# HGRN level products on four column tiles and RWKV state queries inside the state steps of a hybrid decoder layer

## The chip, the cores and the metric

The kernel runs on one core of one Trainium2 chip. Its time is the device time of one execution in microseconds; the runs shown are three of the unchanged kernel. The engines are called by the profile's names: PE is TensorE (PEld its weight loads), DVE VectorE, ACT ScalarE, POOL GpSimd and SP SyncE. The profile comes from one execution of its own.

## The reference

One decoder layer on 2048 tokens of width 1024, all in float32. A joint input projection feeds two mixers that lie side by side: HGRN2 with four heads of 128 columns, and RWKV-7 with eight heads of 64. Their outputs are joined and projected back, and a ConvFFN follows.

```python
def step(S, inp):                        # HGRN2, chunks of 64 tokens
    qb, kb, vb, gb = inp
    b = jnp.cumsum(gb, axis=2)
    diff = b[:, :, :, None, :] - b[:, :, None, :, :]
    dec = jnp.exp(jnp.where(causal, diff, -jnp.inf))
    A = jnp.einsum('bhtk,bhsk,bhtsk->bhts', qb, kb, dec)
    o = jnp.einsum('bhts,bhsv->bhtv', A, vb) + jnp.einsum('bhtk,bhkv->bhtv', qb * jnp.exp(b), S)
    ...

def step(S, inp):                        # RWKV-7, one token
    rt, wt, kt, vt, at, bt = inp
    sa = jnp.einsum('bhvk,bhk->bhv', S, at)
    S = S * wt[:, :, None, :] + sa[..., None] * bt[:, :, None, :] + vt[..., None] * kt[:, :, None, :]
    y = jnp.einsum('bhvk,bhk->bhv', S, rt)
    return S, y
```

RWKV's y is normalised over each head of 64 (mean and variance), scaled by ln_w and shifted by ln_b, gets a bonus term, and is multiplied by a gate.

## The kernel before

The layer is written with a tile framework: the program names tiles and operations, and a planner at build time sets the order of each engine's instructions. It goes by the order of the program and by its own costs, and may put a later instruction first where an earlier one is not ready by those costs. On the chip each engine then runs its own list in order.

The tokens are worked in four blocks of 512. Three generators give out the mixer stage: `dense` (projections, as products of high and low float32r parts, L263 to L265), `rw_stream` (RWKV) and `hg_stream` (HGRN). A loop takes one step of RWKV and one of HGRN and then dense work worth `TICK`, 2000 ns by the program's own costs; call this a round. A step ends at a `yield`.

**HGRN.** `hg_unit` handles one head in one block, 16 times in all. Decay within 128 tokens is handled in seven levels: level l pairs the first half of each group of 2 x 2^l tokens with the second half. `scaled(l)` multiplies queries and keys by the decay that belongs to the level, `level` multiplies them on TensorE (L979), and `take` copies the entries that belong to the level out of PSUM by a mask into the score matrix A (L985). The diagonal (query and key of the same token) is a product of its own. Before the change a block of 64 keys is stationary, 128 rows by 64 columns, and two such blocks go to the two column tiles at columns 0 and 64. Queries that do not take part at a level are skipped, so 32 columns stream past at a level and 64 for the diagonal. Diagonal and levels 0 to 2 form a first run of products, levels 3 to 5 a second; level 6, between the two halves of 128 tokens, is L1023. A is then copied to the two diagonal blocks of Af, whose product with the values is L1041.

**RWKV.** `rw_super` handles two pairs of heads (u = 0, 1; the two heads of a pair lie in partitions 0 to 63 and 64 to 127) in one block, eight times in all. What the change touches:

- Scores (L723): for j in 0, 1 and each pair u, eight products into one PSUM tile (`bank2`, of which two exist), two masked multiplications (L726) that read it, and a `yield`. The multiplication at L711 makes the operand, L712 the one behind it.
- The eight state steps: four state products a step (L894, one for each u and head, 64x64, at the quadrants (0, 0) and (64, 64)) add to `xp`; VectorE scales the result to the next state XH (L896); `yield`.
- The part of y that does not need the state goes to `yp` at L884 beforehand. Behind the eight steps the state queries (L904) add XH times RT to `yp`, 32 products, at the same two quadrants as the state products.
- Then y is squared, averaged by a product with ones on each block of 64, normalised, scaled and shifted by two ScalarE instructions (one for each u), added to the bonus, multiplied by the gate and stored.

A float32 product leaves two records in the trace; a transpose and a float32r product leave one.

Of the kernel before, what the change touches and what calls it, by code (L numbers as in the profile page):

```python
# [7 lines left out]
F32 = mybir.dt.float32  # L8
F32R = mybir.dt.float32r
BF16 = mybir.dt.bfloat16  # L10
U32 = mybir.dt.uint32
AF = mybir.ActivationFunctionType
# [6 lines left out]
P = 128  # L19
# [10 lines left out]

C_CEN, C_ONE, C_S1, C_DG = 0, 128, 256, 384
C_LV = 448
C_SCAN = C_LV + 6 * 64
C_PAR = C_SCAN + 512
C_ID = C_PAR + 2
C_W = C_ID + 128
# [2 lines left out]
def make_consts():  # L39
    import numpy as np  # L40

    c = np.zeros((P, C_W), np.float32)
    p = np.arange(P)[:, None]
    q = np.arange(P)[None, :]
    same = ((p // 64) == (q // 64)).astype(np.float32)
    c[:, C_ID:C_ID + P] = p == q
    for f in range(2):
        c[:, C_PAR + f] = np.arange(P) % 2 == f
    c[:, C_CEN:C_CEN + P] = (p == q) - same / 64.0
    c[:, C_ONE:C_ONE + P] = same  # L50
    t = np.arange(64)[None, :]
    s = p % 64
    c[:, C_S1:C_S1 + 64] = t > s
    c[:, C_S1 + 64:C_S1 + 128] = t >= s
    c[:, C_DG:C_DG + 64] = t == s
    for l in range(6):
        m = 1 << l
        tq = np.arange(64).reshape(-1, 2, m)[:, 1, :].reshape(1, 32)
        c[:, C_LV + 64 * l:C_LV + 64 * l + 32] = ((tq // (2 * m)) == (s // (2 * m))) & ((s // m) % 2 == 0)
    c[:, C_SCAN:C_SCAN + 512] = (np.arange(512) % 64 != 0)[None, :]  # L60
    return c

# [2 lines left out]
def tile_layer(ctx, tc, consts, x, norm1_w, w_in, hg_lb_logits, hg_norm_w, rw_shift_mu, rw_w0, rw_w2,  # L65
# [4 lines left out]
    V, S, TE = nc.vector, nc.scalar, nc.tensor  # L70
    dma, store = nc.sync.dma_start, nc.gpsimd.dma_start

    cp = ctx.enter_context(tc.tile_pool(name="cp", bufs=1, reuse_waits="tile"))
# [16 lines left out]
    blk1 = cst[:, C_ONE:C_ONE + P]  # L90
    s1m = cst[:, C_S1:C_S1 + P]
    dgm = cst[:, C_DG:C_DG + 64]
    scanm = cst[:, C_SCAN:C_SCAN + 512]

    def pst(name):
# [14 lines left out]
    def act(out_, in_, func, **kw):  # L110

        want = tables.get(func)
        if want is not None and want != tab["now"]:
            pre = S.preload_act_table_set(want)
            for u_ in tab["uses"]:
                tc.add_manual_dep(pre.ins, u_.ins.name, NOSYNC, reason="table order")
            tab.update(now=want, pre=pre, uses=[])
        i_ = S.activation(out_, in_, func, **kw)  # L118
        if want is not None:
            tc.add_manual_dep(i_.ins, tab["pre"].ins.name, NOSYNC, reason="table order")  # L120
            tab["uses"].append(i_)
        return i_
# [12 lines left out]
    off = {}  # L135
    with tc.tile_pool(name="vp", bufs=1, reuse_waits="tile") as vp, tc.tile_pool(name="ps0", bufs=1, space=PSUM, reuse_waits="tile") as pools["ps"]:
        rows = vp.tile([P, P], F32, name="rows")
        V.memset(rows, 0.0)
        n = 0
# [15 lines left out]
    def vec(nm, i):  # L155
        return vt[:, off[nm] + i:off[nm] + i + 1]


    lb = cp.tile([P, 12], F32, name="lb")
    lb0 = vt[:, off["lb"]:off["lb"] + 4]  # L160
# [106 lines left out]
    def phase1(c1):  # L267
# [22 lines left out]
        def bank(kind):  # L290
            return ps.tile([P, 512], F32, tag=kind, name=kind, bufs=2)
# [329 lines left out]
        def last_dma(nb):  # L621

            return nc.gpsimd.dma_start if nb == NBLK - 1 else dma
# [16 lines left out]
        def rw_super(nb, s_):  # L640
# [75 lines left out]
            for j in range(2):  # L716
                for u in U:
                    s1 = bank2()
                    for i in range(4):
                        b, e = 2 * j + i // 2, i % 2  # L720
                        for h in range(2):
                            hr = slice(h * 64, h * 64 + 64)
                            TE.matmul(s1[:, h, i * P:i * P + P], KB[hr, 4 * u + b, 2 * e:2 * e + 2, :],  # L723
                                      AR[hr, u, :, 2 * b + e, :], start=True, stop=True)
                    for h in range(2):
                        V.tensor_mul(M[:, :, u, 2 * j:2 * j + 2, h, :].rearrange("p e b t -> p b e t"),  # L726
                                     s1[:, h].rearrange("p (b e t) -> p b e t", e=2, t=P),
                                     s1m.unsqueeze(1).unsqueeze(1).broadcast_to([P, 2, 2, P]))
                    yield

            E = rp.tile([P, 32, 32], F32, tag="E", name="E")
# [148 lines left out]
            for u in U:  # L880
                for ch in range(8):
                    b, e = ch // 2, ch % 2
                    for h in range(2):
                        TE.matmul(yp[h * 64:h * 64 + 64, u, ch * 64:ch * 64 + 64],  # L884
                                  UV[:, 4 * u + b, e, h * 64:h * 64 + 64], M[:, e, u, b, h, 64:128], start=ch == 0,
                                  stop=False, tile_position=(0, h * 64), skip_group_check=True)
            WC2 = WC.rearrange("p (u c) t -> p u c t", u=2)
            for ch in range(8):
                b, e = ch // 2, ch % 2
                cs_ = slice(ch * 64, ch * 64 + 64)  # L890
                for u in U:
                    for h in range(2):
                        hr = slice(h * 64, h * 64 + 64)
                        TE.matmul(xp[hr, u, cs_], M[hr, 1, u, b, e, 0:64], XH[hr, u, ch, :], start=False,  # L894
                                  stop=ch == 7, tile_position=(h * 64, h * 64), skip_group_check=True)
                V.tensor_mul(XH[:, :, ch + 1, :], xp[:, :, cs_], WC2[:, :, ch].broadcast_to([P, 2, 64]))  # L896
                yield
            V.tensor_copy(Xc[:, 2 * s_:2 * s_ + 2, :], XH[:, :, 8, :])
            for u in U:
                for ch in range(8):  # L900
                    cs_ = slice(ch * 64, ch * 64 + 64)
                    for h in range(2):
                        hr = slice(h * 64, h * 64 + 64)
                        TE.matmul(yp[hr, u, cs_], XH[hr, u, ch, :], RT[hr, u, ch, :], start=False, stop=ch == 7,  # L904
                                  tile_position=(h * 64, h * 64), skip_group_check=True)
            yo = tile_("KB", [2, 2, BLK], "yo")
            y1, y2 = yo[:, 0], yo[:, 1]
            act(y1, yp, AF.Square)
# [5 lines left out]
            act(y1, b1, AF.Ln, bias=epsgn, scale=1.0 / 64)  # L914
            act(y1, y1, AF.Exp, scale=-0.5)
            V.tensor_mul(y2, yp, y1)
            for u in U:
                act(y2[:, u], y2[:, u], AF.Identity, bias=vec("lnb", prs[u]), scale=vec("lnw", prs[u]))
            yield
            while ("gd", nb) not in stage:  # L920
                yield None
# [1 line left out]
            gm = bank2()  # L923
            for u in U:
                TE.matmul(gm[:, u, :], g2[:, pc[u]], gdt, start=True, stop=True)
            V.tensor_add(y2, y2, BV)
            V.tensor_mul(y2, gm, y2)
            last_dma(nb)(oT[nb][512 + prs[0] * P:512 + (prs[1] + 1) * P, :].rearrange("(u p) t -> p u t", p=P), y2)
            done["rw2"] += 1
            yield  # L930

# [1 line left out]
        def hg_unit(nb, j):  # L933
# [7 lines left out]
                TE.transpose(tp[:, b * P:(b + 1) * P], v[:, b * P:(b + 1) * P], ident)  # L941
            act(VT, tp.rearrange("p (b t) -> p b t", t=P), AF.Copy)
            yield
            A = rp.tile([P, 4, 64], F32, tag="hA", name="A")
            Pf = f
            Sf = rp.tile([P, BLK], F32, tag="Sf", name="Sf")
            V.memset(Sf.rearrange("p (n e) -> p n e", e=2)[:, :, 1:2], 1.0)
# [18 lines left out]

            def level(lp, off, kt, qt, l=None):

                w = 64 if l is None else 32
                for b in range(4):  # L970
                    for e in range(2):
                        t0 = (2 * b + e) * 64
                        qs = qt[:, t0:t0 + 64]
                        o = lp[e * 64:e * 64 + 64, off + b * w:off + b * w + w]
                        if l is not None:
                            m = 1 << l
                            qs = qs.rearrange("p (n e m) -> p n e m", e=2, m=m)[:, :, 1, :]
                            o = o.rearrange("p (n m) -> p n m", m=m)
                        TE.matmul(o, kt[:, t0:t0 + 64], qs, start=True, stop=True, tile_position=(0, e * 64))  # L979

            def take(l, lp, off):

                m = 1 << l
                mk = cst[:, C_LV + 64 * l:C_LV + 64 * l + 32].bitcast(U32).rearrange("p (n m) -> p n m", m=m)
                V.copy_predicated(A.rearrange("p b (n e m) -> p b n e m", e=2, m=m)[:, :, :, 1, :],  # L985
                                  mk.unsqueeze(1).broadcast_to([P, 4, 32 // m, m]),
                                  lp[:, off:off + 128].rearrange("p (b n m) -> p b n m", b=4, m=m))

            Xs = []
            for l in range(3):  # L990
                Xs.append(scaled(l))
                yield
            l0, l1 = bank("hg"), bank("hg")
            level(l0, 0, k, q)
            for l in range(3):
                level(l1, l * 128, Xs[l], Xs[l], l)
            V.tensor_mul(A, l0[:, 0:256].rearrange("p (b t) -> p b t", t=64), dgm.unsqueeze(1).broadcast_to([P, 4, 64]))
            for l in range(3):
                take(l, l1, l * 128)
            yield  # L1000
            Xs = []
            for l in range(3, 6):
                Xs.append(scaled(l))
                yield
            l1 = bank("hg")
            for l in range(3, 6):
                level(l1, (l - 3) * 128, Xs[l - 3], Xs[l - 3], l)
            for l in range(3, 6):
                take(l, l1, (l - 3) * 128)
            act(Af[0:64, :, 0:64], A[0:64], AF.Copy)  # L1010
            act(Af[64:128, :, 64:128], A[64:128], AF.Copy)
            yield
            X = scaled(6)
            V.tensor_mul(k, k, Sf)
# [587 lines left out]
```

## Time and profile before

| | us |
|---|---|
| runs | 2671.83, 2675.3, 2676.13 (median 2675.3) |
| profiled execution, span from first to last instruction | 2678.7 |
| TensorE busy in the span | 2595.9 (97%) |
| VectorE busy | 1964.4 (73%) |
| ScalarE busy | 1368.4 (51%) |
| HGRN level products (L979, 32 streamed columns), busy | 52.2 |
| HGRN diagonal (L979, 64 columns) | 11.9 |
| RWKV scores (L723) | 37.9 |
| RWKV state products (L894) | 30.2 |
| RWKV state queries (L904) | 18.8 |

For the profiled execution the page gives the span and no other time. Busy time of a group is the union of its instructions' times; products overlap in the pipeline, so a product's own duration (about 0.22 us) is far longer than the distance from one start to the next. In a timeline the columns are start, time covered, engine, line, operation, output and inputs by tile, shapes and count; neighbouring instructions of one kind are merged into one row.

### The profile page before, as it was taken

The numbers are of one execution on the slowest core, as the hardware profiler recorded it, in microseconds if no ns is written. First come the engines' busy times: TensorE is split into PE (matmuls) and PEld (weight loads), VectorE is DVE, ScalarE is ACT, GpSimd is POOL, SyncE is SP. The second block draws the span as 40 slices with busy tenths as digits, with TensorE's granted clock in tenths as the row PEclk, the third lists the DMA queues.
The fourth block names the chain that finished last, engine by engine and source line by source line (L and its number), as shares of the span: only waits on it lengthen the run. The fifth ranks groups of instructions, "written<-read, shape, count | busy, mean of one in ns | idle before, by whom it ended". The sixth has DMA issues, their size and how long they took to land. (4 is left out here: it accounts for less than half of the span.)

```text
span 2678.7 us, 47929 instructions
## 1 busy us (share of the span) xinstructions
PE 2595.9 (97%) x18059; PEld 2089.1 (78%) x18059; DVE 1964.4 (73%) x3744; ACT 1368.4 (51%) x2200; POOL 383.2 (14%) x686
## 2 busy tenths in 40 slices
PE   7999999999999999999999999999999999999998
PEld 5877777777777777778778888887888888888887
DVE  4877767676567675667678789988998888676556
ACT  4556453554545455344457655456555545545444
POOL 6433222212222123222100000000000000000000
PEclk9999999999999999999999999999999999999999
DMA  8654443355643546844584458756754463898665
GB/s 301 202 164 165 163 142 116 115 162 183 201 152 115 153 157 221 277 131 129 172 287 139 138 188 262 239 172 194 260 199 150 149 203 124 318 322 280 204 193 185
DMA packets 312702, 510.54 MB, mean 191 GB/s; under 512 B 46879, under 2 KB 143509, under 8 KB 312469
## 3 DMA queue, kind: packets, MB, share of 16 engines
q1 hardware_dynamic: 257937, 329.13, 37.3%
q0 software_dynamic: 54464, 178.32, 20.4%
q8 instruction: 142, 2.33, 0.4%
q14 instruction: 91, 0.75, 0.1%
q10 hardware_dynamic: 68, 0.02, 0.0%
HBM read 373.13 MB, written 134.22 MB: 189 GB/s over the span
## 5 line engine op out<-in xcount | busy, mean ns | idle before, releaser
L263 PE MATMUL pj<-hh,wh 128*128 128x512 f32 x960 | 394.1, 411 | 6.7 <-ACT rkv L118 1.6
L264 PE MATMUL pj<-hl,wh 128*128 128x512 f32 x960 | 377.9, 394 | 0.0
L265 PE MATMUL pj<-hh,wl 128*128 128x512 f32 x960 | 377.7, 394 | 0.0
L263 PE MATMUL ua<-Bh,uwh 128*128 128x512 f32 x704 | 276.1, 392 | 3.8 <-ACT m L118 2.6
L265 PE MATMUL ua<-Bh,uwl 128*128 128x512 f32 x704 | 274.3, 390 | 0.0
L264 PE MATMUL ua<-Bl,uwh 128*128 128x512 f32 x704 | 274.1, 389 | 0.0
L263 PEld LDWEIGHTS pj<-hh,wh 128*128 128x128 f32 x960 | 181.1, 189 | 56.6 <-issue 9.1
L265 PEld LDWEIGHTS pj<-hh,wl 128*128 128x128 f32 x960 | 181.0, 189 | 39.6 <-issue 0.2
L264 PEld LDWEIGHTS pj<-hl,wh 128*128 128x128 f32 x960 | 181.3, 189 | 34.3 <-issue 0.6
L247 ACT CAST uwh<-uraw 128x512 fp32r<-128x512 f32 x220 | 135.2, 618 | 137.7 <-PE ua L264 63.3
L248 DVE TENSOR_TENSOR dal<-draw,dah 128x512 fp32r<-128x512 f32 x138 | 95.3, 690 | 111.3 <-ACT dah L247 110.0
L248 DVE TENSOR_TENSOR uwl<-uraw,uwh 128x512 fp32r<-128x512 f32 x220 | 147.5, 687 | 35.0 <-ACT uwh L247 34.9
L247 ACT CAST dah<-draw 128x512 fp32r<-128x512 f32 x138 | 85.9, 622 | 163.7 <-PE da L264 79.1
L263 PEld LDWEIGHTS ua<-Bh,uwh 128*128 128x128 f32 x704 | 132.1, 188 | 33.2 <-ACT m L118 4.8
L265 PEld LDWEIGHTS ua<-Bh,uwl 128*128 128x128 f32 x704 | 132.2, 188 | 28.1 <-DVE uwl L248 0.4
L264 PEld LDWEIGHTS ua<-Bl,uwh 128*128 128x128 f32 x704 | 132.2, 188 | 26.8
L263 PE MATMUL ud<-Bh,uwh 128*128 128x512 f32 x352 | 138.0, 392 | 0.0
L265 PE MATMUL ud<-Bh,uwl 128*128 128x512 f32 x352 | 137.0, 389 | 0.0
L264 PE MATMUL ud<-Bl,uwh 128*128 128x512 f32 x352 | 137.0, 389 | 0.0
L1472 POOL DMA_DIRECT2D gd<-y x2 | 1.1, 542 | 945.3 <-DVE y L1470 945.3
L264 PE MATMUL da<-dbl,dah 128*128 128x512 f32 x332 | 129.4, 390 | 0.3 <-DVE dbl L248 0.2
L265 PE MATMUL da<-dbh,dal 128*128 128x512 f32 x332 | 129.2, 389 | 0.0
(580 smaller groups left out, 6268.9 us busy)
## 6 DMA issues: line engine op xcount, KB each, us to landing
uraw<-in_w_up_dram SPq DMA_DIRECT2D x176, 256.0 KB, 3.3
woraw<-in_w_out_dram POOLq DMA_DIRECT2D x96, 256.0 KB, 3.4
br<-gd SPq DMA_DIRECT2D x88, 256.0 KB, 4.0
draw<-Sg SPq DMA_DIRECT2D x88, 256.0 KB, 2.8
draw<-Tw SPq DMA_DIRECT2D x88, 256.0 KB, 3.1
gd<-y SPq DMA_DIRECT2D x86, 256.0 KB, 2.8
Sg<-br SPq DMA_DIRECT2D x72, 256.0 KB, 2.1
xt<-x1d SPq DMA_DIRECT2D x32, 512.0 KB, 6.1
```

The lines of the kernel that those rows point to most:

```text
L247: S.copy(hi, src)
L248: V.tensor_sub(lo, src, hi.bitcast(F32))
L263: TE.matmul(acc, lh, rh, start=first, stop=False, skip_group_check=skip)
L264: TE.matmul(acc, lh, rl, start=False, stop=False, skip_group_check=skip)
L265: TE.matmul(acc, ll, rh, start=False, stop=last, skip_group_check=skip)
L1472: (dma if end is None else nc.gpsimd.dma_start)(gd_[2 * h + b][fb * P:(fb + 1) * P, :], ys[0][:, b * BLK:(b + 1) * BLK])
```

## The change

**HGRN.** A block of 32 keys is now stationary, 128 rows by 32 columns, and four such blocks go to the four column tiles at columns 0, 32, 64 and 96. A level streams 16 queries past each, the diagonal 32. A is 32 columns wide in place of 64. The levels 0 to 4 stay inside such blocks; level 5, between two blocks of 32, becomes `across`, eight products on the column tiles 0 and 64 whose result ScalarE copies from PSUM straight to Af. The diagonal shares a PSUM tile with levels 0 to 2. The masks in the constants shrink in the same way.

**RWKV scores.** For each j both pairs' products and masked multiplications come first, then two yields.

**RWKV state queries.** They move into the state steps, four behind each step's four state products. The second pair's results go to the other column half (`c0 = (h ^ u) * 64`), so the four of a step use all four quadrants, and in `yp` the two heads of the second pair lie exchanged. The scaling by the norm's weights puts them back: two ScalarE instructions of 64 partitions each, with weights exchanged in the same way (`lnx`, copied once at the start). From there y1 takes the place of y2.

```diff
+    lnx = cp.tile([P, 4], F32, name="lnx")
+    for r0 in (0, 64):
+        S.copy(lnx[r0:r0 + 64, :], vt[64 - r0:128 - r0, off["lnw"] + 1:off["lnw"] + 8:2])
...
                         V.tensor_mul(M[:, :, u, 2 * j:2 * j + 2, h, :].rearrange("p e b t -> p b e t"),
...
+                for _ in U:
                     yield
...
-                        TE.matmul(yp[h * 64:h * 64 + 64, u, ch * 64:ch * 64 + 64],
+                        c0 = (h ^ u) * 64
+                        TE.matmul(yp[c0:c0 + 64, u, ch * 64:ch * 64 + 64],
                                   UV[:, 4 * u + b, e, h * 64:h * 64 + 64], M[:, e, u, b, h, 64:128], start=ch == 0,
-                                  stop=False, tile_position=(0, h * 64), skip_group_check=True)
+                                  stop=False, tile_position=(0, c0), skip_group_check=True)
...
+                for u in U:
+                    for h in range(2):
+                        hr, c0 = slice(h * 64, h * 64 + 64), (h ^ u) * 64
+                        TE.matmul(yp[c0:c0 + 64, u, cs_], XH[hr, u, ch, :], RT[hr, u, ch, :], start=False,
+                                  stop=ch == 7, tile_position=(h * 64, c0), skip_group_check=True)
                 V.tensor_mul(XH[:, :, ch + 1, :], xp[:, :, cs_], WC2[:, :, ch].broadcast_to([P, 2, 64]))
                 yield
             V.tensor_copy(Xc[:, 2 * s_:2 * s_ + 2, :], XH[:, :, 8, :])
-            for u in U:
-                for ch in range(8):
-                    cs_ = slice(ch * 64, ch * 64 + 64)
-                    for h in range(2):
-                        hr = slice(h * 64, h * 64 + 64)
-                        TE.matmul(yp[hr, u, cs_], XH[hr, u, ch, :], RT[hr, u, ch, :], start=False, stop=ch == 7,
-                                  tile_position=(h * 64, h * 64), skip_group_check=True)
...
-            for u in U:
-                act(y2[:, u], y2[:, u], AF.Identity, bias=vec("lnb", prs[u]), scale=vec("lnw", prs[u]))
+            act(y1[:, 0], y2[:, 0], AF.Identity, bias=vec("lnb", prs[0]), scale=vec("lnw", prs[0]))
+            for r0 in (0, 64):
+                rs_ = slice(64 - r0, 128 - r0)
+                act(y1[r0:r0 + 64, 1], y2[rs_, 1], AF.Identity, bias=lnx[rs_, 2 + s_:3 + s_], scale=lnx[rs_, s_:s_ + 1])
...
-            A = rp.tile([P, 4, 64], F32, tag="hA", name="A")
+            A = rp.tile([P, 4, 32], F32, tag="hA", name="A")
...
-                w = 64 if l is None else 32
+                w = 32 if l is None else 16
                 for b in range(4):
-                    for e in range(2):
-                        t0 = (2 * b + e) * 64
-                        qs = qt[:, t0:t0 + 64]
-                        o = lp[e * 64:e * 64 + 64, off + b * w:off + b * w + w]
+                    for c0 in range(0, P, 32):
+                        t0 = b * P + c0
+                        qs = qt[:, t0:t0 + 32]
+                        o = lp[c0:c0 + 32, off + b * w:off + b * w + w]
...
-                        TE.matmul(o, kt[:, t0:t0 + 64], qs, start=True, stop=True, tile_position=(0, e * 64))
+                        TE.matmul(o, kt[:, t0:t0 + 32], qs, start=True, stop=True, tile_position=(0, c0))
+
+            def across(lp, off, X):
+
+                for b in range(4):
+                    for c0 in (0, 64):
+                        t0 = b * P + c0
+                        TE.matmul(lp[c0:c0 + 32, off + b * 32:off + b * 32 + 32], X[:, t0:t0 + 32],
+                                  X[:, t0 + 32:t0 + 64], start=True, stop=True, tile_position=(0, c0))
...
-            l0, l1 = bank("hg"), bank("hg")
-            level(l0, 0, k, q)
+            l1 = bank("hg")
+            level(l1, 192, k, q)
             for l in range(3):
-                level(l1, l * 128, Xs[l], Xs[l], l)
+                level(l1, l * 64, Xs[l], Xs[l], l)
...
-            for l in range(3, 6):
-                level(l1, (l - 3) * 128, Xs[l - 3], Xs[l - 3], l)
-            for l in range(3, 6):
-                take(l, l1, (l - 3) * 128)
-            act(Af[0:64, :, 0:64], A[0:64], AF.Copy)
-            act(Af[64:128, :, 64:128], A[64:128], AF.Copy)
+            for l in range(3, 5):
+                level(l1, (l - 3) * 64, Xs[l - 3], Xs[l - 3], l)
+            across(l1, 128, Xs[2])
+            for l in range(3, 5):
+                take(l, l1, (l - 3) * 64)
+            for c0 in (0, 64):
+                act(Af[c0:c0 + 32, :, c0 + 32:c0 + 64],
+                    l1[c0:c0 + 32, 128:256].rearrange("p (b t) -> p b t", t=32), AF.Copy)
+            for c0 in range(0, P, 32):
+                act(Af[c0:c0 + 32, :, c0:c0 + 32], A[c0:c0 + 32], AF.Copy)
```

More of the change, by code (lines that the diff above doesn't have):

```diff
@@ L32 @@
 C_LV = 448
-C_SCAN = C_LV + 6 * 64
+C_D32 = C_LV + 5 * 16
+C_SCAN = C_D32 + 32
 C_PAR = C_SCAN + 512
@@ L55, in make_consts @@
     c[:, C_DG:C_DG + 64] = t == s
-    for l in range(6):
+    s = p % 32
+    for l in range(5):
         m = 1 << l
-        tq = np.arange(64).reshape(-1, 2, m)[:, 1, :].reshape(1, 32)
-        c[:, C_LV + 64 * l:C_LV + 64 * l + 32] = ((tq // (2 * m)) == (s // (2 * m))) & ((s // m) % 2 == 0)
+        tq = np.arange(32).reshape(-1, 2, m)[:, 1, :].reshape(1, 16)
+        c[:, C_LV + 16 * l:C_LV + 16 * l + 16] = ((tq // (2 * m)) == (s // (2 * m))) & ((s // m) % 2 == 0)
+    c[:, C_D32:C_D32 + 32] = np.arange(32)[None, :] == s
     c[:, C_SCAN:C_SCAN + 512] = (np.arange(512) % 64 != 0)[None, :]
@@ L92, in tile_layer @@
     dgm = cst[:, C_DG:C_DG + 64]
+    dg32 = cst[:, C_D32:C_D32 + 32]
     scanm = cst[:, C_SCAN:C_SCAN + 512]
@@ L925, in rw_super @@
                 TE.matmul(gm[:, u, :], g2[:, pc[u]], gdt, start=True, stop=True)
-            V.tensor_add(y2, y2, BV)
-            V.tensor_mul(y2, gm, y2)
-            last_dma(nb)(oT[nb][512 + prs[0] * P:512 + (prs[1] + 1) * P, :].rearrange("(u p) t -> p u t", p=P), y2)
+            V.tensor_add(y1, y1, BV)
+            V.tensor_mul(y1, gm, y1)
+            last_dma(nb)(oT[nb][512 + prs[0] * P:512 + (prs[1] + 1) * P, :].rearrange("(u p) t -> p u t", p=P), y1)
             done["rw2"] += 1
@@ L978, in level @@
                             o = o.rearrange("p (n m) -> p n m", m=m)
-                        TE.matmul(o, kt[:, t0:t0 + 64], qs, start=True, stop=True, tile_position=(0, e * 64))
+                        TE.matmul(o, kt[:, t0:t0 + 32], qs, start=True, stop=True, tile_position=(0, c0))
[5 more added lines that the diff above has]
+                                  X[:, t0 + 32:t0 + 64], start=True, stop=True, tile_position=(0, c0))
             def take(l, lp, off):
                 m = 1 << l
-                mk = cst[:, C_LV + 64 * l:C_LV + 64 * l + 32].bitcast(U32).rearrange("p (n m) -> p n m", m=m)
+                mk = cst[:, C_LV + 16 * l:C_LV + 16 * l + 16].bitcast(U32).rearrange("p (n m) -> p n m", m=m)
                 V.copy_predicated(A.rearrange("p b (n e m) -> p b n e m", e=2, m=m)[:, :, :, 1, :],
-                                  mk.unsqueeze(1).broadcast_to([P, 4, 32 // m, m]),
-                                  lp[:, off:off + 128].rearrange("p (b n m) -> p b n m", b=4, m=m))
+                                  mk.unsqueeze(1).broadcast_to([P, 4, 16 // m, m]),
+                                  lp[:, off:off + 64].rearrange("p (b n m) -> p b n m", b=4, m=m))
             Xs = []
@@ L992, in hg_unit @@
                 yield
-            l0, l1 = bank("hg"), bank("hg")
-            level(l0, 0, k, q)
+            l1 = bank("hg")
+            level(l1, 192, k, q)
             for l in range(3):
-                level(l1, l * 128, Xs[l], Xs[l], l)
-            V.tensor_mul(A, l0[:, 0:256].rearrange("p (b t) -> p b t", t=64), dgm.unsqueeze(1).broadcast_to([P, 4, 64]))
+                level(l1, l * 64, Xs[l], Xs[l], l)
+            V.tensor_mul(A, l1[:, 192:320].rearrange("p (b t) -> p b t", t=32), dg32.unsqueeze(1).broadcast_to([P, 4, 32]))
             for l in range(3):
-                take(l, l1, l * 128)
+                take(l, l1, l * 64)
             yield
```

## Prediction

> **What bounds the kernel now.** I read the page first, then busy time by stage, then what TensorE waited for, and last the order of time around the products that the change touches. The page's first row shows TensorE busy nearly all the time.
>
> ```profile
> PE 2595.9 (97%) x18059; PEld 2089.1 (78%) x18059; DVE 1964.4 (73%) x3744; ACT 1368.4 (51%) x2200; POOL 383.2 (14%) x686
> ```
>
> Busy time by stage (columns: stretch, its length, then busy us and instructions of PE, weight loads, DVE, ACT, POOL; granted clock; DMA share; GB/s) shows where the change lies, and that the granted clock is full. The mixers run up to about 1340 us; behind that come the last output projection and the ConvFFN, which the diff does not touch.
>
> ```profile
> 40.00:1300.00 1260.00, 1216.37 (x11852) 958.98 (x11850) 860.21 (x2046) 614.73 (x977) 338.04 (x604) 0.99 0.51 167
> ...
> 1340.00:2679.00 1339.00, 1320.00 (x5821) 1084.90 (x5819) 1060.85 (x1602) 712.77 (x1147) 16.15 (x30) 1.00 0.64 210
> ```
>
> In the first stretch TensorE is idle for 1260.0 - 1216.4 = 43.6 us, VectorE for 400 and ScalarE for 645. So TensorE is the bound there, as long as its short waits do not grow. The four longest of its waits in that stretch (waited, times, longest single):
>
> ```profile
> PE rw L857 <- ACT M L118: 10.1, 7, 2.2
> PE pj L436 <- ACT hf L118: 4.3, 2, 2.2
> PE rw L1061 <- DVE part L241: 3.6, 5, 1.6
> PE pj L263 <- ACT hh L240: 3.5, 6, 1.1
> ```
>
> They make 21.5 us in 20 waits, 1.08 us each; 43.6 us are then some 40 waits, spread over 1260 us. None of them stands at a product that the change shortens. The rest of the argument is what those products cost on TensorE, and how much of a saving the waits swallow.
>
> **The price of a run of small products.** Each float32 product leaves two records, and small products stand in runs between dense ones. I take a run's net cost as the time from the last dense start before it to the next start after it, less one dense pitch of 0.23 us (114.57 to 114.80 below). The first run of a HGRN unit (16 records of the diagonal, 48 of levels 0 to 2), then the second (48 of levels 3 to 5):
>
> ```profile
> 111.93 0.39 PE L265 MATMUL pj<-hh,wl 128*128 128x512 f32 x1
> 112.25 0.69 PE L979 MATMUL hg<-hq,hk 128*64 128x64 f32 x16
> 112.76 1.54 PE L979 MATMUL hg<-hX 128*64 128x32 f32 x48
> 114.23 0.50 PE L263 MATMUL pj<-hh,wh 128*128 128x512 f32 x1
> 114.57 0.39 PE L264 MATMUL pj<-hl,wh 128*128 128x512 f32 x1
> 114.80 0.40 PE L265 MATMUL pj<-hh,wl 128*128 128x512 f32 x1
> ...
> 122.98 0.39 PE L265 MATMUL pj<-hh,wl 128*128 128x512 f32 x1
> 123.30 1.59 PE L979 MATMUL hg<-hX 128*64 128x32 f32 x48
> 124.82 0.50 PE L263 MATMUL pj<-hh,wh 128*128 128x512 f32 x1
> ```
>
> First run: 114.23 - 111.93 - 0.23 = 2.07 us for 64 records. Second: 124.82 - 122.98 - 0.23 = 1.61 us for 48. The difference gives (2.07 - 1.61) / 16 = 28.8 ns a record and 1.61 - 48 x 0.0288 = 0.23 us for entering and leaving the run. The diagonal's 64 streamed columns take 0.51 us for 16 records (112.25 to 112.76), 32 ns each, hardly more than the 30.6 ns of the levels' 32 columns: how many columns stream past does not set the price. Two other runs show what smaller tiles do:
>
> ```profile
> 142.03 0.39 PE L263 MATMUL pj<-hh,wh 128*128 128x512 f32 x1
> 142.35 0.75 PE L811 MATMUL rw<-TZ,M 32*32 32x32 f32 x64
> 143.03 0.50 PE L264 MATMUL pj<-hl,wh 128*128 128x512 f32 x1
> ...
> 159.34 0.39 PE L265 MATMUL pj<-hh,wl 128*128 128x512 f32 x1
> 159.66 0.69 PE L871 MATMUL rw<-M 64*64 64x64 f32 x32
> 160.17 0.65 PE L871 MATMUL rw<-KBT,M 64*64 64x64 f32 x32
> 160.75 0.50 PE L263 MATMUL pj<-hh,wh 128*128 128x512 f32 x1
> ```
>
> L811 puts 32x32 products on four tiles in turn: 143.03 - 142.03 - 0.23 = 0.77 us, less 0.23 us of switching 0.54 us for 64 records, 8.4 ns each. L871 puts 64x64 products on all four quadrants: 1.41 - 0.23 - 0.23 = 0.95 us, 14.8 ns each. Multiplied by the tiles in use, one tile takes a new record every 28.8 x 2 = 58 ns where 64 columns are stationary, 14.8 x 4 = 59 ns with 64 again, and 8.4 x 4 = 34 ns where 32 are. That is the reading on which the sum stands: price = time of one stationary block, divided by the tiles that work at once.
>
> **HGRN levels.** The groups of HGRN products, with counts (busy us, mean ns):
>
> ```profile
> L979 PE MATMUL hg<-hX 128*64 128x32 f32 x1536 | 52.2, 223 | 0.0
> L979 PE MATMUL hg<-hq,hk 128*64 128x64 f32 x256 | 11.9, 229 | 0.0
> L1023 PE MATMUL hg<-hX 128*64 128x64 f32 x128 | 11.5, 234 | 0.0
> ```
>
> 1536 + 256 records are 16 units of 112. After the change a unit has 4 x 32 = 128 records in its first run, 2 x 32 of levels 3 and 4 and 16 of `across` in its second. No row shows four column tiles that each use all 128 rows. Bounds: 8.4 ns (four tiles at once, L811, which however has 32 rows) and 28.8 ns (the price of every column-tiled row with 128 rows here). I take 8.4: L811's pace comes of its 32 stationary columns, and rows seem not to count, since 128 rows (L979) and 64 rows (L871) give the same 58 ns a tile. `across` uses two column tiles, 34 / 2 = 16.8 ns. First run: 128 x 0.0084 + 0.23 = 1.31 us against 2.07. Second: 64 x 0.0084 + 16 x 0.0168 + 0.23 = 1.04 against 1.61. A unit saves 1.33 us, 16 units **21.3 us**.
>
> **State-query products.** Now one run of 64 records per pair of heads, on the two diagonal quadrants:
>
> ```profile
> 191.30 0.40 PE L265 MATMUL pj<-hh,wl 128*128 128x512 f32 x1
> 191.63 2.08 PE L904 MATMUL rw<-AR,XH 64*64 64x64 f32 x64
> 193.64 1.16 PE L1032 MATMUL hg<-VT,KT 128*128 128x128 f32 x8
> ```
>
> That is 2.34 - 0.23 = 2.11 us. Afterwards eight of them follow each state product run (L894) directly, in the same tile mode and on four quadrants, at L871's price: 64 x 14.8 ns = 0.95 us and no switch of their own. They read XH[ch], which the state product ahead of them has already waited for, so they add no wait; VectorE's L896 needs the state products alone. 8 x 1.16 = **9.3 us**; bounds 8 x 0.23 = 1.8 us (only the switch) and 9.3.
>
> **Scores.** Two runs of 16 records become one of 32, if they stay together.
>
> ```profile
> 230.18 0.39 PE L265 MATMUL pj<-hh,wl 128*128 128x512 f32 x1
> 230.50 1.16 PE L723 MATMUL rw<-AR,KB 64*128 64x128 f32 x16
> 231.59 0.50 PE L263 MATMUL pj<-hh,wh 128*128 128x512 f32 x1
> ...
> 233.86 1.16 PE L723 MATMUL rw<-AR,KB 64*128 64x128 f32 x16
> ...
> 86.26 0.39 PE L264 MATMUL pj<-hl,wh 128*128 128x512 f32 x1
> 86.58 2.06 PE L723 MATMUL rw<-AR,KB 64*128 64x128 f32 x32
> 88.56 0.50 PE L265 MATMUL pj<-hh,wl 128*128 128x512 f32 x1
> ```
>
> Alone a run costs 1.41 - 0.23 = 1.18 us; the one fused pair in the trace 2.30 - 0.23 = 2.07. A fusion saves 0.29 us, and there are two for each of eight passes: 4.6 us. Against it stands a wait: the second pair's PSUM tile comes free only when L712 is done, the multiplication behind L711, which releases the first pair.
>
> ```profile
> L712 DVE TENSOR_TENSOR BV<-rw,rkv 128x1024 f32<-128x1024 f32 x8 | 9.8, 1219 | 0.0
> ...
> L118 ACT ACTIVATE Af<-A 64x256 f32<-64x256 f32 x32 | 13.2, 414 | 19.1 <-DVE A L985 18.8
> ...
> L118 ACT ACTIVATE yo<-yo,vt 128x512 f32<-128x512 f32 x16 | 12.2, 811 | 3.5 <-DVE yo L916 3.5
> ```
>
> The first run of 0.94 us covers most of 1.22, so 8 x 0.28 = 2.2 us may be waited, with the dense products behind it in TensorE's queue. I take 4.6 - 2.2 = **2.4 us**; bounds 4.6 and a loss of 2.2.
>
> **Costed at nothing.** VectorE's takes and the diagonal multiplication handle half as many columns, one level less, so VectorE only gets lighter. ScalarE gets six Af copies in place of two, at most 4 x 0.41 x 16 = 26 us, and three scalings by the norm's weights in place of two, 0.81 x 8 = 6.5 us. It is busy 615 of 1260 us; Af is read three rounds later (L1041), at least 6 us of dense fill. Were that cover gone, as in the last unit and pass, 4 x 0.41 + 0.81 = 2.5 us would show once. Two copies for lnx come once, behind the same transpose for which everything else waits. The yields of each generator keep their number, so the dense fill is dealt out as before, and no DMA is moved past another in the program.
>
> **Sum.** 21.3 + 9.3 + 2.4 = 33.0 us of TensorE time. A saving in a round that ends in a wait is eaten by that wait. A round is 233.86 - 230.50 = 3.36 us, and 40 of them are 134 us, 11% of the stretch; so 29.4 us reach the end. The profiled execution would be 2678.7 - 29.4 = 2649.3. Its span lies 3.4 us above the median of the runs, so the runs give 2675.3 - 29.4 = **2646**.
>
> **A rule that speaks against it.** The Trainium skill, "TensorE: Matmul & The Clock Gate", section "Wait — 56ns, not 53.3ns?", says that two matmuls never start less than about 25 ns apart, however little each streams; more and smaller products would then cost more. The trace disagrees: L811 starts 64 records within 0.68 us. By the rule 208 records a unit would take 5.2 us and the whole change would end some 25 us later, at about 2700.
>
> **Rivals.**
> (A) Four column tiles with 128 rows work only two at a time, 16.8 ns a record. First run 128 x 0.0168 + 0.23 = 2.38 us, second 1.58: 0.28 us lost a unit, 4.5 in all. 9.3 + 2.4 - 4.5 = 7.2, 89% of it 6.4: 2669. For it: no row has more than two column tiles on the same rows. Against: two such tiles already halve the price of one (L1023, one tile, 11.5 us for 128 records, is 90 ns with its switch).
> (B) Half the saving turns into waits, since rounds get shorter and ScalarE's and VectorE's chains do not: 16.5 us, 2659. For it: L857's seven waits. Against: both engines idle a third or more of the stretch.
> (C) The change does not do what it says: the planner, which orders by its own costs, sets dense products between the scores and between state and query products as now between L723's runs. Then HGRN's 21.3 alone, 19: 2656.
> (D) Slower. A record that uses all 128 rows keeps its 28.8 ns whatever its columns, as if such records were served one by one. 208 x 28.8 + 0.46 = 6.45 us a unit against 3.68, 44.3 us in all, less 1.8 and 2.4: 2715. It decides from the price at which 208 records a unit eat the other gains: (3.68 + 11.7 / 16 - 0.46) / 208 = 19 ns. For it: no 128-row record in the trace is cheaper. Against: L1023 and L979, with the same rows, differ by the number of tiles. The floor that the Trainium skill states, above, would be this rival at 25 ns; no row here bears it out.
>
> **Chances.** Forecast 64% (2636 to 2656), B 12%, C 8%, A 8%, D 5%, other things 3%. The low end is everything saved, 35.2 us with no loss, 2640, and the spread of runs with a shorter tail below it: 2634. The high end takes in B, C and half of A: 2668. About 0.2%, 5 us, is what a measurement of this kernel can tell from no change. Below 2670 lie the forecast, B, C and half of A: 89%; within 5 us 5%; slower 6%.
>
> **What would show it.** HGRN's products as 32-column records, 128 in the first run at about 1.3 us net and 80 in the second at 1.0: right; 2.4 and 1.6: A; 3.9 and 2.5: D. L894's runs followed at once by query products, no 64-record run left, and 0.7 us from dense to dense growing by about 0.12. L723 in runs of 32. Idle TensorE time from 40 to 1300 of 44 to 50 us; 60 would be B. The stage behind 1340 us keeps its 1339 us. The prediction is wrong if the time does not fall below 2668, or if the runs have these prices and the stage is no shorter.

## The result and the profile after

The changed kernel took 2661.1 us (median of five runs, 2657.2 to 2665.3) against 2675.3: a ratio of 0.9943, 95% interval 0.9927 to 0.996, or 15 us faster. The forecast was 2646, 29 us faster; 2661.1 lies above its main range (2636 to 2656) and inside the outer one (up to 2668). The profiled execution spans 2660.8 us against 2678.7. The page's row for the engines, after:

```profile
PE 2560.2 (96%) x19595; PEld 2061.2 (77%) x19595; DVE 1952.9 (73%) x3728; ACT 1389.2 (52%) x2274; POOL 380.4 (14%) x686
```

TensorE's busy time fell by 2595.9 - 2560.2 = 35.7 us, twice what the span fell (17.9 us). So the first reading is: the work went away as forecast, and half of it came back as idle time. The runs of small products, in TensorE's timeline:

```profile
109.91 0.39 PE L272 MATMUL pj<-hh,wl 128*128 128x512 f32 x1
110.22 0.46 PE L988 MATMUL hg<-hq,hk 128*32 128x32 f32 x32
110.50 1.03 PE L988 MATMUL hg<-hX 128*32 128x16 f32 x96
111.46 0.50 PE L270 MATMUL pj<-hh,wh 128*128 128x512 f32 x1
...
120.21 0.39 PE L272 MATMUL pj<-hh,wl 128*128 128x512 f32 x1
120.53 0.72 PE L988 MATMUL hg<-hX 128*32 128x16 f32 x63
...
121.10 0.43 PE L995 MATMUL hg<-hX 128*32 128x32 f32 x15
121.46 0.50 PE L270 MATMUL pj<-hh,wh 128*128 128x512 f32 x1
...
171.37 0.39 PE L272 MATMUL pj<-hh,wl 128*128 128x512 f32 x1
171.69 0.39 PE L903 MATMUL rw<-XH,M 64*64 64x64 f32 x6
171.87 0.27 PE L908 MATMUL rw<-AR,XH 64*64 64x64 f32 x2
171.91 0.22 PE L903 MATMUL rw<-XH,M 64*64 64x64 f32 x2
171.97 0.28 PE L908 MATMUL rw<-AR,XH 64*64 64x64 f32 x6
172.19 0.50 PE L270 MATMUL pj<-hh,wh 128*128 128x512 f32 x1
...
227.44 0.39 PE L272 MATMUL pj<-hh,wl 128*128 128x512 f32 x1
227.76 2.06 PE L730 MATMUL rw<-AR,KB 64*128 64x128 f32 x32
229.75 0.50 PE L270 MATMUL pj<-hh,wh 128*128 128x512 f32 x1
```

By the prediction's rule (dense start to next start, less 0.23 us) HGRN's first run costs 111.46 - 109.91 - 0.23 = 1.32 us (forecast 1.31, before 2.07), the second 1.02 (1.04, before 1.61). A state step with its four queries, dense to dense, is 172.19 - 171.37 = 0.82 us, where 0.70 plus 0.12 was forecast; the 64-record query run is gone. Scores come in runs of 32 records at 2.08 us net in 13 of 16 places; in three, other products stand between them. The idle time is seen by stage, in the columns that the prediction explains. Before:

```profile
40.00:1260.00 1220.00, 1176.93 (x11207) 927.95 (x11206) 825.95 (x1955) 593.62 (x939) 329.41 (x588) 0.99 0.52 168
```

After:

```profile
40.00:1260.00 1220.00, 1161.32 (x12919) 915.52 (x12918) 836.30 (x2001) 627.98 (x1034) 331.77 (x597) 0.99 0.52 170
```

TensorE idles for 58.7 us of the same stretch in place of 43.1. The eight largest groups of its waits there, after (waited, times, longest single):

```profile
PE rw L865 <- ACT M L122: 6.7, 6, 2.1
PE hg L1063 <- DVE SH L1055: 5.1, 3, 4.1
PE pj L270 <- ACT hh L247: 4.3, 4, 1.4
PE hg L1042 <- DVE hk L1035: 4.1, 4, 1.6
PE pj L443 <- ACT hf L122: 4.1, 2, 2.1
PE rw L832 <- ACT ZT L122: 3.3, 5, 1.4
PE pj L270 <- ACT rkv L122: 3.3, 2, 1.7
PE pj L270 <- DVE xh L413: 2.9, 4, 1.5
```

Before, three groups of waits on VectorE made 10.1 of 11.7 us, L1061's 3.6 that the prediction shows and these two:

```profile
PE hg L1021 <- DVE hk L1014: 3.4, 1, 3.4
PE pj L264 <- DVE wl L248: 3.1, 6, 1.9
```

Now waits on VectorE add up to 24.0 us, and those on ScalarE stay at 28 to 29. The first stretch in which an HGRN unit meets the RWKV recurrence (from the first L792 or L800 to the transposes that end it) shows VectorE taking over as the bound. Before, then after:

```profile
109.30:141.30 32.00, 31.96 (x254) 26.42 (x253) 30.23 (x109) 11.21 (x21) 14.58 (x25) 1.00 0.59 194
```

```profile
107.60:136.00 28.40, 26.81 (x334) 22.04 (x333) 27.37 (x101) 9.05 (x20) 12.96 (x22) 1.00 0.62 200
```

Before, TensorE had no gap in it and VectorE 1.8 us; after, VectorE is busy 27.4 of 28.4 us and TensorE idles 1.6, all of it in one wait of L1042 on VectorE's L1035. The recurrence is 31 dependent steps of two short VectorE instructions. This stretch is one of the tightest. Over the eight recurrences (first to last L792 or L800, 264.2 us before and 240.4 after) VectorE is busy 88% before and 90% after, and TensorE's idle time rises from 6.6 to 12.3 us; in the 50 us behind each of them it rises from 19.1 to 30.3 us in all. So most of the new idle time lies in and just behind the recurrences.

### The profile page after: what moved, and what is told of

The parts are those of the page before. It is cut to its first block, busy times and chain, and to the rows that moved or that the text cites. A ratio compares the mean times of both kernels' runs of the same rounds, so it can differ in the third digit from the quotient of the medians.

```text
span 2660.8 us, 51050 instructions
## 1 busy us (share of the span) xinstructions
PE 2560.2 (96%) x19595; PEld 2061.2 (77%) x19595; DVE 1952.9 (73%) x3728; ACT 1389.2 (52%) x2274; POOL 380.4 (14%) x686
```

## The experiments

Three theories were set against each other. **V**: VectorE's recurrence, covered before by TensorE's work, now makes TensorE wait. **W**: any saving is halved by short waits that are everywhere. **I**: the denser runs outrun the fetch of TensorE's instructions. All ratios are to the kernel before, and "us" is (ratio - 1) x 2675.

| kernel | ratio (95% interval) | us |
|---|---|---|
| levels alone | 0.9960 (0.9945 to 0.9976) | -10.7 |
| queries alone | 0.9985 (0.9971 to 1.0) | -4.0 |
| scores alone | 0.9997 (0.9986 to 1.0008) | -0.8 |
| whole change | 0.9943 (0.9927 to 0.996) | -15.2 |
| before, recurrence cut short | 0.9998 (0.9987 to 1.0008) | -0.5 |
| levels alone, cut short | 0.9939 (0.9924 to 0.9954) | -16.3 |
| queries alone, cut short | 0.9955 (0.9938 to 0.9971) | -12.0 |
| whole change, cut short | 0.9877 (0.9857 to 0.9896) | -32.9 |
| before, VectorE work to ScalarE and GpSimd | 1.0035 (1.0021 to 1.0049) | +9.4 |
| whole change, the same | 0.9962 (0.9948 to 0.9977) | -10.2 |
| whole change, two VectorE instructions to GpSimd | 0.9975 (0.9963 to 0.9988) | -6.7 |
| whole change, 2100 ns of dense work a round | 0.9977 (0.9964 to 0.999) | -6.2 |
| whole change, 2200 ns | 0.9949 (0.9934 to 0.9965) | -13.6 |

**One part at a time.** Each kernel is the one before with one part of the diff: the hunks of `hg_unit` and its masks; the hunks of the state steps, `lnx` and the scaling; or this:

```diff
+                for _ in U:
                     yield
```

> The kernel before with the HGRN part alone (32-key blocks, across, narrower A). TensorE time saved by the prices of the two traces: 21 us. Theory V (VectorE sets the pace where the RWKV recurrence L792/L794 and an HGRN unit are emitted in the same rounds, so what TensorE saves there becomes waits): about half of the units lie in such rounds, 8 to 12 us faster than before, and this part carries nearly all of the loss. Theory W (a saving anywhere is halved, because short waits are everywhere): 10 to 11 us. Theory I (the denser runs outrun the fetch of TensorE's instructions): 14 to 17 us, since issue waits grew by 4 us.

> The kernel before with the state queries inside the state steps, the exchanged second pair and its scaling, nothing else. TensorE time saved: 9.3 us. V: the state steps are not in the recurrence's rounds, so 7 to 9 us faster. W: about 4.5. I: 9.

> The kernel before with both pairs' scores in one run, nothing else. TensorE time saved at most 4.6 us. V and I: 3 to 4.6 us faster. W: about 2. If the masked multiplications, four in a row, delay others on VectorE, 0 or slower.

Measured 10.7, 4.0 and 0.8 us, together 15.5 against 15.2 for the whole. By these times each part lost about half of its TensorE time (21.3, 9.3, 4.6) or more, as W had said. The traces do not bear W out. TensorE's idle time over the whole profiled span is 82.8 us in the kernel before, 85.6 with the levels alone, 82.1 with the queries, 79.1 with the scores, and 100.6 with the whole change: alone, no part brought more than 3 us of idle time. I falls as the main cause: waits of TensorE for its own instructions ("issue") up to 1260 us are 0.4, 0.8 and 1.7 us with one part and 3.4 with the whole change, against 1.4 before.

What the edited kernels share is a lower granted clock: 0.992 to 0.994 in most runs, where most runs of the kernel before have 0.994 to 0.996. Within one kernel the time goes with it: the changed one took 2665.3 us at 0.991 and 2657.2 at 0.994. So runs of equal clock should be compared (mean us, number of runs in brackets):

| granted clock | before | levels | queries | scores | whole | before, cut short | whole, cut short |
|---|---|---|---|---|---|---|---|
| 0.993 | 2678.6 (3) | 2663.8 (3) | 2671.9 (5) | 2673.3 (6) | 2660.0 (1) | 2676.8 (3) | none |
| 0.994 | 2676.6 (13) | 2662.7 (2) | 2667.2 (2) | 2670.7 (1) | 2657.2 (1) | 2672.9 (7) | 2643.5 (2) |

At equal clock the levels gain 14 to 15 us, the queries 7 to 9 and the scores 5 to 6, together 27 to 29, which is nearly the forecast; the whole change gains 19. By this reading the parts do not add up: queries and scores keep most of their saving alone, and much of the loss comes when the parts stand together. Some cells hold one run, so these figures are good to a few us only. Since waits can themselves lower the clock (last section), the comparison may also take out a part of what they cost. The last two columns belong to the next experiment.

**The recurrence cut short.** 29 of its 31 steps are left out, in the kernel before and in the changed one, so VectorE has less to do and the triangular inverse is incomplete:

```diff
-                V.tensor_mul(tv, E[:, j, j + 1:32]...
-                V.tensor_add(Ti[:, j + 1:32, 0:ncol], ...
+                if j < 2:
+                    V.tensor_mul(tv, E[:, j, j + 1:32]...
+                    V.tensor_add(Ti[:, j + 1:32, 0:ncol], ...
```

> The kernel before, with 2 of the recurrence's 31 steps (L792, L794) and the other 29 left out, yields kept: some 117 us less on VectorE, TensorE's products all there. The control for the next run. All theories: some 10 to 25 us faster than before, as far as VectorE held TensorE up.

> The changed kernel with the same 29 steps left out. V: the gap to the control opens to 27 to 33 us, nearly all of the 33 to 35 us of TensorE time. W: it stays at half, 15 to 18 us. I: 17 to 22 us, since the fetch of instructions does not ask for VectorE.

The control gained nothing (0.9998), against my expectation of 10 to 25 us; at equal clock it is 2 to 4 us ahead. In the kernel before, then, TensorE covered the recurrence but for a few us. The changed kernel without those steps is 32.4 us (0.9998 - 0.9877) ahead of its control, against 33 us of TensorE time that the prediction had worked out, and twice the 15.2 us with the recurrence in place. By the intervals the difference of 17 us is good to some 7 either way. W and I had said 15 to 22. At a clock of 0.994 the two gaps are 29.4 and 19.4 us, so about 10 us hang on the recurrence there, and some of the 17 goes with the clock. The two stretches, first the short control, then the short changed kernel:

```profile
40.00:1260.00 1220.00, 1178.83 (x11232) 931.82 (x11231) 749.90 (x1531) 595.73 (x945) 330.08 (x590) 0.99 0.51 168
```

```profile
40.00:1260.00 1220.00, 1172.59 (x13376) 926.94 (x13374) 757.70 (x1566) 635.32 (x1045) 337.26 (x603) 0.99 0.53 172
```

VectorE has 76 to 79 us less in each (87 and 91 over the whole span, where I had expected 117). TensorE's idle time is 41.2 us in the control, 2 less than in the full kernel before, and 47.4 in the short changed kernel, 11 less than in the full one. So the change adds 15.6 us of idle time with the recurrence in place and 6.2 without it. What is left of the waits on VectorE there adds up to 14.6 us and is led by other lines; the wait on hk (L1035), 4.1 us in the full kernel, is gone from the list, and SH is down to one wait (lines behind the recurrence have numbers one higher in this kernel):

```profile
PE hg L1083 <- DVE part L248: 3.4, 2, 3.2
PE rw L1083 <- DVE part L248: 2.6, 4, 1.3
PE pj L270 <- DVE xh L413: 2.6, 4, 1.2
PE pj L271 <- DVE wl L255: 2.4, 7, 1.0
PE hg L1064 <- DVE SH L1056: 1.6, 1, 1.6
```

**Which part pays.** The same cut with one part each:

> The HGRN part alone, with 29 of the recurrence's 31 steps left out, to be held against the kernel before with the same steps left out (0.9998 of the kernel before). V (this part lost half of its 21 us to VectorE's recurrence): 18 to 22 us faster than that control. W, or the clock that fell in most edited kernels as the whole cause: 10 to 13 us, as with the recurrence in place.

> The state queries alone, with the same 29 steps left out, against the same control. V in its first form (the recurrence's own rounds): the state steps are in other rounds, so 4 us as with the recurrence in place. V in a wider form (the recurrence also leaves VectorE late in the rounds behind it): 7 to 9 us. W: 4 us.

Against the control the levels gain 0.9998 - 0.9939 = 15.8 us in place of 10.7, the queries 11.5 in place of 4.0. So by the times the recurrence cost both parts, the queries too, which the wider form of V had said (the recurrence leaves VectorE late in the rounds behind it); the levels stay short of their 21 us. But each of the two differences, 5.1 and 7.5 us, is good to some 6.5 either way only, and 11.5 us is more than the queries' 9.3 us of TensorE time. How the loss divides between the parts is not settled.

**VectorE made lighter without leaving work out.** If VectorE's load were the whole matter, taking some away should help. First, f's scale and shift and k = 1 - f on ScalarE and a memset on GpSimd, in both kernels:

```diff
-                V.tensor_scalar(t_, t_, lb[:, 4 + j:5 + j], lb[:, j:j + 1], ALU.mult, ALU.add)
+                act(t_, t_, AF.Identity, bias=lb[:, j:j + 1], scale=lb[:, 4 + j:5 + j])
...
-            V.tensor_scalar(k, f, -1.0, 1.0, ALU.mult, ALU.add)
+            act(k, f, AF.Identity, bias=1.0, scale=-1.0)
...
-            V.memset(Sf.rearrange(
+            nc.gpsimd.memset(Sf.rearrange(
```

> The kernel before with 1.2 us of VectorE work per HGRN unit put elsewhere (f's scale and shift and k = 1 - f as ScalarE instructions, Sf's memset on GpSimd), the same result. V: 3 to 7 us faster than before, less than the next run gains over the changed kernel. W and I: within 3 us of before.

> The changed kernel with the same work put elsewhere. V: 6 to 12 us faster than the changed kernel, 2649 to 2655. W and I: within 3 us of the changed kernel.

Neither gained, a clear miss of V's expectation: the first became 9.4 us slower, and the second's 5 us against the changed kernel lie within the intervals. In the first of them VectorE's waits hold a new entry:

```profile
DVE hf L963 <- ACT hk L118: 15.6, 5, 6.5
```

k now comes from ScalarE's queue behind evictions of the projections, and VectorE waits 15.6 us for it, as much as the 8.7 + 6.8 = 15.5 us of work that it was spared for f and k in 16 units. TensorE's waits on VectorE up to 1260 us grew from 11.7 to 18.4 us. Second, work whose consumer comes rounds later, to GpSimd, in the changed kernel:

```diff
-            V.tensor_mul(q, q, Pf)
+            nc.gpsimd.tensor_mul(q, q, Pf)
...
-            V.tensor_copy(Sc[:, j, :], SH[:, 4, :])
+            nc.gpsimd.tensor_copy(Sc[:, j, :], SH[:, 4, :])
```

> The changed kernel with two VectorE instructions of an HGRN unit on GpSimd, both with a consumer some rounds later: q times the decay (0.69 us on VectorE) and the state's copy to Sc (0.22). 14.6 us less on VectorE, the same result. V (waits on VectorE eat 12 us of the saving): 3 to 10 us faster than the changed kernel, 2651 to 2658. If GpSimd's queue of weight loads holds them up, or the planner's order moves as it did with the first relief: equal or up to 8 us slower. W: within 3 us of the changed kernel.

It too became slower, by 8.5 us against the changed kernel. GpSimd takes 1.3 to 4.1 us for what VectorE did in 0.69:

```profile
L1036 POOL TENSOR_TENSOR hq<-hq,hf x16: 1287/1764/4082, 125.7 to 1290.7; 128x512 f32<-128x512 f32 x16
```

and TensorE's largest group of waits on VectorE grew from 5.1 us to this:

```profile
PE hg L1063 <- DVE SH L1055: 9.4, 4, 5.9
```

Nothing is recorded as waiting for the moved multiplication, and VectorE waited 1.3 us in all for the moved copy, so whether GpSimd's slowness or the planner's new order did it stays open.

**Longer rounds.**

```diff
-TICK = 2000.0
+TICK = 2100.0
```

> The changed kernel with 2100 ns of dense work a round in place of 2000, so that a round has about the TensorE work that it had before. V: the waits on VectorE shrink by a third or more, 2650 to 2657. W: no difference beyond 3 us. If the planner's order matters more than the length of a round, either sign by up to 10 us.

> The changed kernel with 2200 ns a round. V: 2645 to 2657, unless the dense work now ends before the RWKV chain and the last passes stand open, which costs up to 20 us. W: no difference beyond 3 us, or slower by the open end.

With 2100 the kernel is 9 us slower than the changed kernel, with 2200 the same within the intervals. V's forecast missed in both: up to 1260 us TensorE's waits on VectorE are 24.3 and 25.7 us, where the changed kernel has 24.0. The 9 us go with the clock, which was 0.986 to 0.992 with 2100: its one run at 0.992 took 2661.4 us, and the changed kernel's two at 0.992 took 2661.9 on average. No kernel that computes the reference beat the changed one.

## Why the prediction came out as it did

The ratio of what was forecast to what came is 29 to 15. Step by step:

- **Prices of the runs: right.** A first run of 128 records on four column tiles, with 128 rows each, costs 1.32 us, within 0.01 of the forecast from 8.4 ns a record. Rival A (two tiles at a time, 2.38 us) and rival D (28.8 ns a record, 3.92 us) fall. The floor of 25 ns between starts that the Trainium skill states ("TensorE: Matmul & The Clock Gate", "Wait — 56ns, not 53.3ns?") would by an estimate have made it 128 x 25 ns = 3.2 us; here the 32 records of the diagonal, on four tiles, take 0.28 us from 110.22, 8.8 ns each.
- **Queries: right in TensorE's time.** 0.12 us more a step, no run of their own, and 1.2 us of waits on the state's scaling (L910) where it was 1.0.
- **Scores: right.** Runs of 32 records in 13 of 16 places, no wait for PSUM worth noting. Rival C falls.
- **Costed at nothing: VectorE's lightening did not help.** "VectorE only gets lighter" was right in its sum (1952.9 us in place of 1964.4), yet in the stretch shown above it became the bound (27.4 of 28.4 us).
- **"So 29.4 us reach the end": the step that failed.** I let waits swallow 11% of the saving, by counting the rounds that already ended in a wait. That leaves out the rounds in which another engine was just covered. Idle TensorE time up to 1260 us rose by 15.6 us, where 3.6 was forecast for the whole, and over the span by 17.8. The prediction's own sign points the same way: from 40 to 1300 us it had put 44 to 50 us of idle time for itself and 60 for rival B, and 64.3 came. I had read VectorE's room as an average (400 of 1260 us idle); in the recurrence's stretch of 32 us it had 1.8, beside a TensorE without a gap.
- **The granted clock: left out of the sum.** I called it full, and so it was in the kernel before (0.995). The changed one has 0.992. At equal clock the gain is 19 us in place of 15, so about 4 us of the missing 14 go with the clock.
- **Rival B** (half the saving turns into waits, 2659) is what happened, as far as the profiled pair goes. I had named L857's waits on ScalarE for it; it was VectorE's. That its number fits within 2 us is partly luck, since the clock's share was in no rival.
- **Two sums are wrong.** Below 2670 lie 64 + 12 + 8 + 4 = 88%, not 89. The 2700 by the rule of 25 ns leaves out the switching of 0.46 us a unit and the gains of queries and scores; with both it would be 2675 + 16 x 1.98 - 11.7 = 2695. Neither changes the forecast.

Shown is that a good part of the loss goes when the recurrence goes: without it the change gives 32.4 us, with it 15.2 (29 and 19 at equal clock), while the kernel before moves by 4 us at most. Not shown is a single late result that carries it, nor that a lighter VectorE would win it back; none of the attempts gained. Leaving out steps changes the planner's order too, and the moved instructions above shifted the time by up to 9 us, so a share of the order in the 17 us is a rival that no run here separates. What lowers the clock of the edited kernels is open as well.

## What to carry to other kernels

Before counting a saving on a busy engine, look in the same stretch for a second engine with hardly a gap: its room there, and not its average over the stage, says how much can be saved before it takes over as the bound. A saving that shows as less busy time and an equal span is best traced by leaving out the suspected cover in both kernels: if the old kernel hardly changes and the new one runs ahead, the cover is the likely cause, as far as the order of the rest stays. Where the granted clock differs between runs by as little as 0.002, hold runs of equal clock against each other before dividing a few us among causes. Moving work to an engine with time to spare helps only if it does not put that engine's queue into a chain that was short.

## What the runs showed of the hardware

**A run of products stopped in its middle.** In the first run of the last HGRN unit of the changed kernel TensorE stood still for 2.06 us without waiting for another engine:

```profile
1272.49 0.92 PE L988 MATMUL hg<-hX 128*32 128x16 f32 x82
1275.47 0.31 PE L988 MATMUL hg<-hX 128*32 128x16 f32 x14 [2.06 <-issue]
```

In that gap the DMA view of 1273 to 1275.5 us has one packet in an instruction queue:

```profile
q8 instruction: 1, 0.02, 2.4%
```

Waits of this kind ("issue") made 1.4 us before 1340 us in the kernel before and 5.5 in the changed one, so they are a small part of the loss. That TensorE had run out of instructions and this packet brought them is inferred from its time, not shown.

**Waits can be paid twice.** Behind that gap, and from 1290.1 us on, the granted clock stood at one half for 3.4 us and 6.8 us (the number before the last two):

```profile
1276.50:1279.90 3.40, 3.40 (x23) 2.34 (x21) 1.36 (x6) 0.62 (x1) 0.00 (x0) 0.50 0.02 5
1290.10:1296.90 6.80, 5.75 (x15) 4.14 (x16) 2.81 (x5) 3.20 (x6) 0.00 (x0) 0.50 0.61 205
```

In the 3.4 us ahead of the first stretch TensorE was busy for 1.3 us, ahead of the second for 1.95. The second has no gap above 1 us ahead of it, only waits of 0.3 and 0.9 us and the first 0.2 us of a wait of 1.27. At half clock dense products started 0.43 us apart in place of 0.23:

```profile
1292.16 0.63 PE L270 MATMUL pj<-wh,hh 128*128 128x512 f32 x1
1292.59 0.63 PE L272 MATMUL pj<-wh,hl 128*128 128x512 f32 x1
1293.02 0.63 PE L271 MATMUL pj<-wl,hh 128*128 128x512 f32 x1
```

The Trainium skill ("TensorE: Matmul & The Clock Gate", "What's actually happening") puts the half clock behind an idle window of about 3.4 us; the stretches here have that length or twice it, but a gap of 2.06 us was enough. Over the timed runs the mean granted clock was 0.995 in the kernel before (0.993 to 0.998) and 0.992 in the changed one (0.991 to 0.994); 0.3% of 2660 us would be 8 us, and the runs of equal clock above put about 4 on it. It can't be separated from the waits themselves: medians of the edited kernels are 0.992 to 0.994 whether faster or slower, apart from the longer rounds with 0.988 and 0.990.
